# Pairs of tiles in a Strassen feed-forward: their input combinations taken apart into two halves, decode rows first, two products of the second column block ahead of the first block's third

## The chip, the cores and the metric

The kernel runs on one core of a Trainium2 chip. The metric is the device time of one execution in microseconds (us). Five engines work beside each other, each with its own in-order instruction queue: TensorE (PE; PEld is its weight load), VectorE (DVE), ScalarE (ACT), GpSimd (POOL) and SyncE (SP, which here only issues DMAs). The order of each queue is fixed when the program is built, by a planner that works from the order of the program text and from estimated times; an instruction then waits in its queue for the semaphores of what it needs.

## The reference, cut to what matters

Two layers of an encoder work on 1,024 prompt rows and 128 decode rows (8 streams of 16), together 9 tiles of 128 rows by 1,024 columns. A layer is a mixer, an output projection with a norm, and a gated feed-forward with a causal convolution of width 3:

```python
x = layer_norm(ALPHA * x + (mix @ w_out), ln1_g, ln1_b)
hg = x @ w_gate
hu = x @ w_up
ext = jnp.concatenate([conv_prev, hg], axis=1)
conv = conv_b + sum(conv_w[j] * ext[:, j:j + t] for j in range(CONV_W))
x = layer_norm(ALPHA * x + (jax.nn.gelu(conv) * hu) @ w_down, ln2_g, ln2_b)
```

`w_gate` and `w_up` are 1,024 by 2,816. All is float32 and has to stay nearly exact, so each operand is split in a high part (a cast to TensorE's float32r) and a low part (the operand less its high part), and each product is three matmuls (`mm3`, lines 176 to 178): high by high, high by low, low by high.

## The kernel before

**The feed-forward as seven products.** The two weights of a block of 128 columns (`f` = 0 to 21) and the two halves of the rows form a 2 by 2 block product, done in Winograd's form of Strassen with seven products in place of eight: A11 by B11, A12 by B21, S2 by T2, S1 by T1, S4 by B22, S3 by T3, A22 by T4. The A and S are weights and sums of weights, made anew for each block. The B and T are inputs, made once for each layer: B11 and B21 are the two column halves of tiles 0 to 3 and half of the decode tile, B22 is the second column half of tiles 5 to 8 and the other half of the decode tile, and the T combine them. The first row half is in tiles 0 to 3 (group `G1` with the decode tile 4), the second in tiles 5 to 8 (`G2`); tile `j` of the second is paired with tile `j - 5` of the first. Each operand is 128 by 4 by 576, high and low; `product` (line 1379) makes one product in 24 matmuls of 288 columns, each k-step by the three of `mm3`, into one PSUM tile of two banks out of four such tiles (`banks`).

**Before the feed-forward.** The output projection goes over four column slabs; with the last (`s` = 3) each tile of G2 is normalised (`norm_rows`, then `affine_rows`: line 233 multiplies by the gain, line 234 adds the bias, on the two engines that `NORM1` names for the tile) and stored to `x1d`. `VP` means multiply on DVE and add on POOL, `VV` both on DVE. The decode tile and tiles 0 to 3 were turned (transposed by TensorE) and split by `half1` while the projection still ran.

**The pairs.** `pair(j, where)` turns tile `j` (line 1238, eight matmuls, into a PSUM tile named trx, halves va and vb), copies va into a buffer t3 (line 1276), and makes t1 = va - B11 by two POOL subtractions (lines 1261 and 1262; high part, then low part), B22 from vb, t2 = vb - t1 and t3 = vb - va on DVE (lines 1279, 1280), T1 and T2 by splitting t1 and t2 (`put`: line 1228 on ACT makes the high part, line 1229 the low part), t2 = B21 - t2 by two POOL operations (lines 1266, 1267), and T3 and T4 by splitting t3 and t2. The three buffers t1 (in `tail`), t2 and t3 are the same for all four pairs. `pair_dec` does the same for the decode rows on POOL, with the same buffers, after the four pairs. In the text, product A11 of block 0 stands ahead of the pairs, A12 of block 0 between the second and third pair, and everything else after `pair_dec`.

**Weights.** `wnext` makes the next weight operand of a list `wops` in the order of use and splits it (line 1341 on ACT, 1342 on DVE) into one of eight slots of `ring`; the slots are handed round, so one is free when the product that used it is over. The sums S take POOL operations (lines 1335 to 1337 for S2, of which the first writes `tail` and S1 is split from it; line 1339 for S4). Raw weights come by SP in halves of 512 KB (`raw_load`) into two buffers. Eight `wnext` come ahead of the pairs, and each product later calls one more.

**The loop over blocks.** For each `f`: seven products; s1 is copied from the first (line 1502), `gate_in` and `add` take the others out of PSUM on DVE, `conv` and `gated` finish the block, and it is stored to `ad`. The down-projection loads it again from there (`load_a`, two buffers).

Of the kernel before, what the change touches and what calls it, by code (L numbers as in the profile page):

```python
# [10 lines left out]
F32 = mybir.dt.float32  # L11
# [10 lines left out]
P = 128  # L22
# [7 lines left out]
NF = 22  # L30
# [37 lines left out]
def hybrid_encoder(ctx: ExitStack, tc: tile.TileContext, d: dict):  # L68
    nc = tc.nc
# [64 lines left out]
    plan = []  # L134
    MOVER = nc.vector
    PP, VV, VP = (nc.gpsimd, nc.gpsimd), (nc.vector, nc.vector), (nc.vector, nc.gpsimd)
    NORM1 = 5 * [VP] + 4 * [VV]
    NORM2 = [6 * [VP] + 3 * [VV], 8 * [VP] + [VV]]
    for L in range(d["layers"]):
        plan.append((d["w_v"][L], nc.vector if L == 0 else nc.gpsimd))  # L140
# [49 lines left out]
    tail = arp.tile([P, 640], F32, name="tail")  # L190
# [83 lines left out]
    for L in range(d["layers"]):  # L274
# [13 lines left out]
        for q, tl in enumerate(SETS):  # L288
            n = len(tl)
# [542 lines left out]
        for p in range(3):  # L832
# [16 lines left out]
            st = {}  # L849
# [293 lines left out]
        xp1 = pool(f"xp1_{L}", 1, st=fst)  # L1143
        hx = xp1.tile([P, 1170], F32, name="hx")
        ct = [xp1.tile([P, 1152], F32, name="ct0")]
        xg1s = ExitStack()
        xpg = pool(f"xpg_{L}", 1, st=xg1s)
        for j in G1:
# [50 lines left out]
        arb = opr.tile([P, 4608], F32R, name="arb")  # L1199
        xs2 = ExitStack()  # L1200
        xp2 = pool(f"xp2_{L}", 1, st=xs2, right=True)
        temps = [tail[:, 0:512]] + [xp2.tile([P, 512], F32, name=f"temp{n}") for n in range(2)]
        x12d = xp2.tile([P, 4, 2, 32], F32, name="x12d")
        for j in G2:
            x1s[j] = xp2.tile([P, D], F32, name=f"x1_{j}")
            nc.sync.dma_start(x1s[j], x_src[j])
# [3 lines left out]
        def operand(t, n):  # L1210
            return t[:, 4608 * n:4608 * n + 4608].rearrange("p (a k n) -> p a k n", a=2, k=4)

        opx = {"B11": operand(ar, 0), "B21": operand(ar, 1), "T3": operand(ar, 2), "T4": operand(ar, 3),
               "B22": operand(ara, 0), "T1": operand(arb, 0)}
        def temp():
            temps.append(temps.pop(0))
            return temps[-1]

        def cols_of(i):

            if i < 4:
# [4 lines left out]
        def put(at, n, src, eng):  # L1226

            nc.scalar.copy(at(n, 0), src)  # L1228
            eng.tensor_tensor(at(n, 1), src, at(n, 0).bitcast(F32), ALU.subtract)

        def turned_x(src, where):

            out = []
            for c in range(2):
                b = where(c)
                bv = b.rearrange("p (k t) -> p k t", k=4)
                for k in range(4):
                    nc.tensor.transpose(bv[:, k, :], src[:, (4 * c + k) * P:(4 * c + k + 1) * P], ident)
                out.append(bv)
            return out  # L1240
# [18 lines left out]
        def sub2(at, t, n, src, e):  # L1259

            e[0].tensor_tensor(t, src, at(n, 0).bitcast(F32), ALU.subtract)
            e[1].tensor_tensor(t, t, at(n, 1).bitcast(F32), ALU.subtract)

        def rsub2(at, t, n, src, e):

            e[0].tensor_tensor(t, at(n, 0).bitcast(F32), src, ALU.subtract)
            e[1].tensor_tensor(t, t, at(n, 1).bitcast(F32), ALU.add)
# [2 lines left out]

        def pair(j, where):

            va, vb = turned_x(x1s[j], where)
            at = cols_of(j - 5)
            t1, t2, t3 = (temp().rearrange("p (k t) -> p k t", k=4) for _ in range(3))
            nc.scalar.copy(t3, va)
            sub2(at, t1, "B11", t3, (G, G))
            put(at, "B22", vb, V)
            V.tensor_tensor(t2, vb, t1, ALU.subtract)
            V.tensor_tensor(t3, vb, t3, ALU.subtract)  # L1280
            put(at, "T1", t1, V)
            put(at, "T2", t2, V)
            rsub2(at, t2, "B21", t2, (G, G))
            put(at, "T3", t3, V)
            put(at, "T4", t2, V)

        def pair_dec():
            at = cols_of(4)
            t1, t2, t3 = (temp()[:, :256].rearrange("p (k c t) -> p k c t", k=4, c=2) for _ in range(3))
            sub2(at, t1, "B11", x12d, (G, G))  # L1290
            put(at, "T1", t1, G)
            rsub2(at, t2, "B22", t1, (G, G))
            put(at, "T2", t2, G)
            rsub2(at, t3, "B22", x12d, (G, G))
            put(at, "T3", t3, G)
            rsub2(at, t2, "B21", t2, (G, G))
            put(at, "T4", t2, G)

        def norm1(j):
            if j in G2:  # L1300
# [6 lines left out]
        aw = {}  # L1307
        raws = {}
        wops = [(n, f) for f in range(NF) for n in ("A11", "A12", "S2", "S1", "S4", "S3", "A22")]

        def wslot(k):
            return ring[:, 1024 * k:1024 * k + 512], ring[:, 1024 * k + 512:1024 * k + 1024]

        def raw_load(f, a):
            r = rawp.tile([P, 1184], F32, tag="raw", name="raw")
            nc.sync.dma_start(r[:, :1024], d["w_gu"][L, f, :, 1024 * a:1024 * a + 1024])
            raws[f, 2 * a], raws[f, 2 * a + 1] = r[:, 0:512], r[:, 512:1024]

        def wnext():


            i = wnext.i
            if i == len(wops):
                return
            wnext.i += 1
            n, f = wops[i]
            if n == "A11" and f == 0:
                raw_load(0, 0)
                raw_load(0, 1)
            if n == "A12" and f > 0:  # L1330
                raw_load(f, 1)
            a11, a12, a21, a22 = (raws.get((f, c)) for c in range(4))
            src = {"A11": a11, "A12": a12, "S1": tail[:, 0:512], "S2": a11, "S3": a21, "S4": a12, "A22": a22}[n]
            if n == "S2":
                G.tensor_tensor(tail[:, 0:512], a21, a22, ALU.add)
                G.tensor_tensor(a21, a11, a21, ALU.subtract)
                G.tensor_tensor(a11, tail[:, 0:512], a11, ALU.subtract)
            if n == "S4":
                G.tensor_tensor(a12, a12, a11, ALU.subtract)
            h, l = wslot((4 + i) % 8)  # L1340
            nc.scalar.copy(h, src)  # L1341
            V.tensor_tensor(l, src, h.bitcast(F32), ALU.subtract)  # L1342
            aw[n, f] = h.rearrange("p (k n) -> p k n", k=4), l.rearrange("p (k n) -> p k n", k=4)
            if n == "S4" and f < NF - 1:
                raw_load(f + 1, 0)

        wnext.i = wnext.late = 0

# [15 lines left out]
        t2p = pool(f"t2p{L}", 1, st=fst)  # L1364
        art = t2p.tile([P, 4608], F32R, name="art")
        opx["T2"] = operand(art, 0)
        for _ in range(4):
            wnext()
        pst.close()
# [29 lines left out]
        def where():  # L1399
            t = banks("trx")  # L1400
            return lambda c: t[:, c, :]

        first = [product("A11", 0, "B11")]
        pair(5, where())
        pair(6, where())
        first.append(product("A12", 0, "B21"))
        pair(7, where())
        pair(8, where())
        pair_dec()
        turn1.clear()  # L1410
        for _ in range(wnext.late):
            wnext()
# [5 lines left out]
        nc.sync.dma_start(stc, d["st_conv"][L])  # L1418
        tails = fp.tile([P, NF, 16], F32, name="tails")
        tailp = fp.tile([P, NF, 2], F32, name="tailp")  # L1420
        as_ = ExitStack()
        asp = pool(f"as{L}", 2, st=as_, right=True)
        gs_ = ExitStack()
        gsp = pool(f"gs{L}", 1, st=gs_, right=True)
        ct.append(gsp.tile([P, 1152], F32, name="ct1"))
        s1, s2, s3 = (gsp.tile([P, 2, 288], F32, name=n) for n in ("s1", "s2", "s3"))
        nc.gpsimd.memset(hx[:, 0:2], 0.0)

        def halves_of(t, h):
# [35 lines left out]
        def load_a(f):  # L1465
            o = 2304 * ((f + 2) % 8)
            ah, al = ar[:, o:o + 1152], ar[:, o + 1152:o + 2304]
            for c in range(2):
                s_ = slice(576 * c, 576 * c + 576)
                rw = asp.tile([P, 576], F32, tag="araw", name="araw")  # L1470
                nc.sync.dma_start(rw, ad[f][:, s_])
                nc.scalar.copy(ah[:, s_], rw)  # L1472
                V.tensor_tensor(al[:, s_], rw, ah[:, s_].bitcast(F32), ALU.subtract)
            avs[f] = (ah, al)
# [19 lines left out]

        for f in range(NF):
            end = f == NF - 1
            b1, b2 = first if f == 0 else (product("A11", f, "B11"), product("A12", f, "B21"))
            if end:
                load_a(0)
                load_w(0, 0)  # L1500
            G.tensor_copy(dv[:, :, 0:2], stc[:, f, :].rearrange("p (b t) -> p b t", b=8))
            nc.scalar.copy(s1, b1[:, :, :288])
            gate_in(f, 0, s1, b2)
            add(s1, s1, product("S2", f, "T2"))
            if end:
                load_a(1)
                load_w(0, 1)
            add(s2, s1, product("S1", f, "T1"))
            gate_in(f, 1, s2, product("S4", f, "B22"))
            conv(f)  # L1510
            b7 = product("S3", f, "T3")
            add(s2, s2, b7)
            add(s3, s1, b7)
            gated(f, 1, s2)
            add(s3, s3, product("A22", f, "T4"))
            gated(f, 0, s3)
            nc.scalar.dma_start(ad[f], ct[f % 2])


        gs_.close()  # L1520
        as_.close()
        ops_.close()
        pst.close()
        pst = ExitStack()
# [3 lines left out]
        ws_ = ExitStack()  # L1528
        ac1 = pool(f"ac1_{L}", 1, st=ws_, right=True)
        acc = [(ac1 if j in G1 else ac2).tile([P, D], F32, name=f"acc{j}") for j in range(NT)]  # L1530
        asp = pool(f"at{L}", 2, st=ws_, right=True)
        wsp = pool(f"ws{L}", 1, st=ws_, right=True)
        wdv["x"] = wsp.tile([P, 4 * 1024], F32R, name="wdx")
        gt, bt = hx[:, :D], ct[0][:, :D]
# [231 lines left out]
```

## Time and profile before

| | |
|---|---|
| time, median of 3 runs | 2965.39 us (2965.12 to 2967.64) |
| profiled execution, its own time | 2963.75 us |
| its span in the trace | 2961.9 us |
| PE busy | 2791.9 us, 94% of the span |
| PE weight load busy | 2616.6 us, 88% |
| DVE busy | 2072.2 us, 70% |
| ACT busy | 1375.6 us, 46% |
| POOL busy | 937.4 us, 32% |
| mean granted clock of PE | 0.972 of full speed |

The table is to be read as a sum over stages: a share of 94% means that PE stood still for 170 us of the span, and where these lie is not in the table. The page's 40 slices (74 us each) show PE at 9 tenths or more but for a few, among them the one around 700 us and the one around 2170 us, which hold the pairs of the first and of the second layer.

### The profile page before, as it was taken

What the parts mean: (1) busy time and instruction counts of PE and PEld (TensorE: products, weight loads), DVE (VectorE), ACT (ScalarE), POOL (GpSimd) and SP (SyncE); (2) the same over time, 40 slices, a digit from 0 to 9 for tenths busy, and PEclk for the clock granted to TensorE, in tenths of its full rate; (3) what the DMA queues carried; (4) which work ended last, traced back from release to release, by engine and by line L of the source; (5) the groups of instructions that cost most, each with busy time, mean ns of one, the idle gap of its engine ahead of it and who ended that gap; (6) DMA issues with size and microseconds to landing.
All of it is one profiled execution on the core that took longest, in us unless ns stands there. A gap on an engine that the chain in (4) does not pass through costs nothing.

```text
span 2961.9 us, 51451 instructions
## 1 busy us (share of the span) xinstructions
PE 2791.9 (94%) x19412; PEld 2616.6 (88%) x19412; DVE 2072.2 (70%) x4706; ACT 1375.6 (46%) x2881; POOL 937.4 (32%) x927
## 2 busy tenths in 40 slices
PE   9999999994999999999998999989959999999998
PEld 8888898994999999788898988989959999997886
DVE  6899778765666666554678996787656666665646
ACT  6588556543333333411255884666433333334211
POOL 3334443445223222000433455334352322310003
PEclk9999999997999999999999999999979999999999
DMA  4111123131222222533112111131312222234411
GB/s 139 53 60 48 41 65 105 53 132 45 75 78 72 75 75 87 165 129 111 72 51 83 36 53 39 54 112 53 132 45 75 75 75 74 76 104 139 160 64 64
DMA packets 100981, 239.95 MB, mean 81 GB/s; under 512 B 20710, under 2 KB 41086, under 8 KB 100734
## 3 DMA queue, kind: packets, MB, share of 16 engines
q1 hardware_dynamic: 83982, 195.38, 20.4%
q10 hardware_dynamic: 16752, 41.29, 3.6%
q8 instruction: 153, 2.51, 0.3%
q14 instruction: 94, 0.77, 0.1%
HBM read 181.99 MB, written 54.64 MB: 80 GB/s over the span
## 4 chain that ended last, share of the span: by engine, by line
PE 77%; DVE 11%; DMA 3%; issue 3%; POOL 3%; ACT 2%; SPq 0%; ACTq 0%; DVEq 0%; POOLq 0%
PE pg L178 11%; PE pg L176 11%; PE pg L177 11%; PE pdn L176 6%; PE pdn L178 6%; PE pdn L177 6%; PE pwo L176 2%; PE pwo L178 2%; PE pwo L177 2%; PE pvg L176 2%; PE pvg L177 2%; PE pvg L178 2%; PE tp L989 1%; DVE spare L562 1%; DMA raw<-w_d 1%
## 5 line engine op out<-in xcount | busy, mean ns | idle before, releaser
L176 PE MATMUL pg<-ar,ring 128*128 128x288 f32 x1408 | 414.6, 294 | 1.1 <-DVE x L1160 1.1
L178 PE MATMUL pg<-ar,ring 128*128 128x288 f32 x1408 | 415.3, 295 | 0.0
L177 PE MATMUL pg<-ar,ring 128*128 128x288 f32 x1408 | 414.5, 294 | 0.0
L1341 ACT CAST ring<-raw 128x512 fp32r<-128x512 f32 x264 | 163.6, 620 | 454.8 <-PE pg L177 417.9
L128 POOL TENSOR_TENSOR ring<-raw,ring 128x512 fp32r<-128x512 f32 (+1 forms) x140 | 193.7, 1409 | 323.2 <-ACT ring L127 275.6
L1342 DVE TENSOR_TENSOR ring<-raw,ring 128x512 fp32r<-128x512 f32 x264 | 204.5, 775 | 110.5 <-ACT ring L1341 106.9
L568 ACT ACTIVATE spare<-sc,cand 128x384 bf16<-128x384 f32 (+4 forms) x262 | 244.3, 932 | 74.7 <-DVE cand L594 30.4
L176 PEld LDWEIGHTS pg<-ar,ring 128*128 128x128 f32 x1408 | 264.1, 188 | 1.3 <-issue 1.3
L178 PEld LDWEIGHTS pg<-ar,ring 128*128 128x128 f32 x1408 | 264.1, 188 | 0.0
L177 PEld LDWEIGHTS pg<-ar,ring 128*128 128x128 f32 x1408 | 264.1, 188 | 0.0
L1597 DVE TENSOR_TENSOR acc<-acc,pdn 128x512 f32<-128x512 f32 x180 | 122.8, 684 | 179.3 <-PE pdn L178 178.0
L1493 DVE TENSOR_TENSOR s<-s,pg 128x576 f32<-128x576 f32 x220 | 164.2, 748 | 53.6 <-PE pg L178 50.9
L1437 DVE TENSOR_TENSOR hx<-s,pg 128x512 f32<-128x512 f32 x88 | 60.5, 688 | 154.5 <-PE pg L178 153.1
L176 PE MATMUL pwo<-ring,ar 128*128 128x256 f32 x576 | 167.1, 290 | 0.0
L178 PE MATMUL pwo<-ring,ar 128*128 128x256 f32 x576 | 164.0, 285 | 0.0
L177 PE MATMUL pwo<-ring,ar 128*128 128x256 f32 x576 | 164.0, 285 | 0.0
L562 DVE TENSOR_SCALAR_CACHE_REDUCE spare<-sc,cand 128x384 bf16<-128x384 f32 (+3 forms) x208 | 158.2, 761 | 1.4
L176 PE MATMUL pg<-art,ring 128*128 128x288 f32 x352 | 104.5, 297 | 51.1 <-ACT art L1228 51.1
L1472 ACT CAST ar<-araw 128x576 fp32r<-128x576 f32 x88 | 58.9, 675 | 198.7 <-PE pdn L177 107.0
L176 PE MATMUL pdn<-ring,ar 128*128 128x512 f32 x360 | 140.9, 391 | 2.9 <-DVE s L1493 2.9
L178 PE MATMUL pdn<-ring,ar 128*128 128x512 f32 x360 | 140.8, 391 | 0.0
L177 PE MATMUL pdn<-ring,ar 128*128 128x512 f32 x360 | 140.7, 391 | 0.0
(403 smaller groups left out, 9533.5 us busy)
## 6 DMA issues: line engine op xcount, KB each, us to landing
raw<-w_gu SPq DMA_DIRECT2D x88, 512.0 KB, 3.7
ad<-ct ACTq DMA_DIRECT2D x44, 576.0 KB, 2.8
araw<-ad SPq DMA_DIRECT2D x88, 288.0 KB, 3.6
raw<-w_d SPq DMA_DIRECT2D x44, 512.0 KB, 4.4
raw<-w_s SPq DMA_DIRECT2D x40, 512.0 KB, 3.9
raw<-w_o SPq DMA_DIRECT2D x32, 512.0 KB, 4.1
x1d<-x ACTq DMA_DIRECT2D x18, 512.0 KB, 2.7
ml<-mixd SPq DMA_DIRECT2D x18, 320.0 KB, 3.2
```

The lines of the kernel that those rows point to most:

```text
L128: eng.tensor_tensor(l[:, t], raw[:, r], h[:, t].bitcast(F32), ALU.subtract)
L176: nc.tensor.matmul(out, lh, rh, start=first, stop=False)
L177: nc.tensor.matmul(out, lh, rl, start=False, stop=False)
L178: nc.tensor.matmul(out, ll, rh, start=False, stop=last)
L562: nc.vector.tensor_scalar(junkv[:, :w], sc[i], cand[q][:, c:c + 1].bitcast(F32), float(kof(i) - w), op0=ALU.is_lt, op1=ALU.add, accum_out= ...
L568: nc.scalar.activation(junka[:, :w], sc[i], AF.Sign, bias=cand[q][:, c:c + 1].bitcast(F32), scale=-1.0, accum_out=dst)
L1341: nc.scalar.copy(h, src)
L1342: V.tensor_tensor(l, src, h.bitcast(F32), ALU.subtract)
L1437: V.tensor_tensor(hp.rearrange("p (c n) -> p c n", c=2), prompt(sv), prompt(b), ALU.add)
L1472: nc.scalar.copy(ah[:, s_], rw)
L1493: V.tensor_tensor(out, a, b[:, :, :288], ALU.add)
L1597: V.tensor_tensor(acc[j][:, cs], acc[j][:, cs], po, ALU.add)
```

## The change

It takes the pairs' work apart and moves it. `pair` now ends after T2 and T1 and returns a function `rest` (B21 - t2, and T3 and T4), which is called after all four pairs. t1 stays in `tail`; t2 and t3 of the first pair are two new buffers, those of each later pair are the two halves of the tile of the pair before. For the last pair (`j` = 8) the two subtractions for t1 are on DVE. `pair_dec` moves ahead of the pairs, into the end of the output projection, with a buffer of its own (x4d); its T3 and T4 splits follow the pairs. Products A11 and A12 of block 1 are made between the pairs, and `wops` has their weights third and fourth; the raw weights come in another order, and the half that holds A11 and A12 of block 1 is read twice. s1 is copied right after the first product and has a place of its own. The bias adds of tiles 5, 6 and 7 go from DVE to POOL. In the down-projection one of `load_a`'s two buffers is s1.

```diff
-    NORM1 = 5 * [VP] + 4 * [VV]
+    NORM1 = 8 * [VP] + [VV]
...
+        s1 = xp1.tile([P, 2, 288], F32, name="s1")
...
-            t1, t2, t3 = (temp().rearrange("p (k t) -> p k t", k=4) for _ in range(3))
+            t1, t2, t3 = (t.rearrange("p (k t) -> p k t", k=4) for t in (tail[:, 0:512], *temps))
+            temps[:] = x1s[j][:, 0:512], x1s[j][:, 512:1024]
+            e = V if j == 8 else G
             nc.scalar.copy(t3, va)
-            sub2(at, t1, "B11", t3, (G, G))
+            sub2(at, t1, "B11", t3, (e, e))
             put(at, "B22", vb, V)
             V.tensor_tensor(t2, vb, t1, ALU.subtract)
             V.tensor_tensor(t3, vb, t3, ALU.subtract)
+            put(at, "T2", t2, V)
             put(at, "T1", t1, V)
-            put(at, "T2", t2, V)
-            rsub2(at, t2, "B21", t2, (G, G))
-            put(at, "T3", t3, V)
-            put(at, "T4", t2, V)
+
+            def rest():
+                rsub2(at, t2, "B21", t2, (G, G))
+                put(at, "T3", t3, V)
+                put(at, "T4", t2, V)
+
+            return rest
 
         def pair_dec():
             at = cols_of(4)
-            t1, t2, t3 = (temp()[:, :256].rearrange("p (k c t) -> p k c t", k=4, c=2) for _ in range(3))
+            t1 = tail[:, :256].rearrange("p (k c t) -> p k c t", k=4, c=2)
             sub2(at, t1, "B11", x12d, (G, G))
             put(at, "T1", t1, G)
-            rsub2(at, t2, "B22", t1, (G, G))
-            put(at, "T2", t2, G)
-            rsub2(at, t3, "B22", x12d, (G, G))
-            put(at, "T3", t3, G)
-            rsub2(at, t2, "B21", t2, (G, G))
-            put(at, "T4", t2, G)
+            rsub2(at, x4d, "B22", t1, (G, G))
+            put(at, "T2", x4d, G)
+            rsub2(at, x12d, "B22", x12d, (G, G))
+            rsub2(at, x4d, "B21", x4d, (G, G))
+
+        def rest_dec():
+            at = cols_of(4)
+            put(at, "T3", x12d, G)
+            put(at, "T4", x4d, G)
...
+        wops[2:9] = wops[7:9] + wops[2:7]
...
-            if n == "A11" and f == 0:
+            if i == 0:
+                raw_load(1, 0)
                 raw_load(0, 0)
-                raw_load(0, 1)
-            if n == "A12" and f > 0:
-                raw_load(f, 1)
...
+            if i == 3:
+                raw_load(0, 1)
             if n == "S4" and f < NF - 1:
                 raw_load(f + 1, 0)
+            if n == "A22" and f < NF - 1:
+                raw_load(f + 1, 1)
...
+        pair_dec()
         for _ in range(4):
             wnext()
...
-        first = [product("A11", 0, "B11")]
-        pair(5, where())
-        pair(6, where())
-        first.append(product("A12", 0, "B21"))
-        pair(7, where())
-        pair(8, where())
-        pair_dec()
+        first = {f: [] for f in range(2)}
+        rests = []
+
+        def early(f, n, x):
+            first[f].append(product(n, f, x))
+
+        early(0, "A11", "B11")
+        nc.scalar.copy(s1, first[0][0][:, :, :288])
+        rests.append(pair(5, where()))
+        early(0, "A12", "B21")
+        rests.append(pair(6, where()))
+        early(1, "A11", "B11")
+        rests.append(pair(7, where()))
+        early(1, "A12", "B21")
+        rests.append(pair(8, where()))
+        rest_dec()
+        for r in rests:
+            r()
...
-                rw = asp.tile([P, 576], F32, tag="araw", name="araw")
+                rw = s1.rearrange("p c n -> p (c n)") if f > 1 and c else asp.tile([P, 576], F32, tag="araw", name="araw")
```

## Rows read from the trace of the kernel before

**Rows 1.** Waits of PE, 655 to 725 us: total us, times, longest.

```profile
PE pg L176 <- ACT art L1228: 25.6, 1, 25.6
PE trx L1238 <- ACT art L1228: 12.5, 2, 7.7
```

**Rows 2.** Stretches: length, busy (count) of PE, PEld, DVE, ACT, POOL; clock, DMA, GB/s.

```profile
680.00:700.00 20.00, 1.94 (x8) 1.56 (x8) 12.57 (x20) 8.46 (x15) 11.40 (x9) 0.50 0.00 0
700.00:720.00 20.00, 10.85 (x64) 10.86 (x65) 6.51 (x8) 5.69 (x11) 16.34 (x19) 0.64 0.01 2
720.00:740.00 20.00, 20.00 (x152) 20.00 (x152) 15.23 (x24) 9.01 (x13) 7.14 (x7) 1.00 0.32 111
```

**Rows 3.** Timeline of PE: start, us, instruction, [idle before].

```profile
662.11 1.95 PE L1238 MATMUL trx<-identr,x 128*128 128x128 f32 x16
...
671.97 1.94 PE L1238 MATMUL trx<-identr,x 128*128 128x128 f32 x8 [4.74 <-ACT art L1228]
...
709.15 0.61 PE L176 MATMUL pg<-art,ring 128*128 128x288 f32 x1 [25.57 <-ACT art L1228]
...
733.87 0.29 PE L176 MATMUL pg<-art,ring 128*128 128x288 f32 x1
...
2183.38 0.61 PE L176 MATMUL pg<-art,ring 128*128 128x288 f32 x1 [25.56 <-ACT art L1228]
...
2208.25 0.29 PE L176 MATMUL pg<-art,ring 128*128 128x288 f32 x1
```

**Rows 4.** Timeline of ACT in the same stage.

```profile
645.45 0.62 ACT L1341 CAST ring<-tail 128x512 fp32r<-128x512 f32 x1 [0.71 <-PE pwo L177]
...
674.85 0.59 ACT L1276 COPY temp<-trx 128x512 f32<-128x512 f32 x1 [2.37 <-DVE ar L1229]
...
683.38 0.59 ACT L1276 COPY temp<-trx 128x512 f32<-128x512 f32 x1 [1.23 <-DVE ar L1229]
...
708.69 0.41 ACT L1228 CAST art<-temp 128x256 fp32r<-128x256 f32 x1 [2.31 <-POOL temp L1267]
```

**Rows 5.** Timeline of DVE.

```profile
672.35 1.21 DVE L234 TENSOR_TENSOR x<-x,ct 128x1024 f32<-128x1024 f32 x1
...
675.96 0.69 DVE L1229 TENSOR_TENSOR ara<-trx,ara 128x512 fp32r<-128x512 f32 x1 [1.20 <-ACT ara L1228]
679.01 1.09 DVE L1229 TENSOR_TENSOR ar<-temp,ar 128x512 fp32r<-128x512 f32 x1 [2.36 <-ACT ar L1228]
680.20 0.69 DVE L1279 TENSOR_TENSOR temp<-trx,tail 128x512 f32<-128x512 f32 x1
680.81 0.68 DVE L1280 TENSOR_TENSOR temp<-trx,temp 128x512 f32<-128x512 f32 x1
...
699.06 0.69 DVE L1229 TENSOR_TENSOR art<-temp,art 128x512 fp32r<-128x512 f32 x1
```

**Rows 6.** Timeline of POOL.

```profile
613.84 2.40 POOL L234 TENSOR_TENSOR x<-x,ct 128x1024 f32<-128x1024 f32 x1 [4.24 <-DVE x L233]
...
640.33 1.29 POOL L1335 TENSOR_TENSOR tail<-raw 128x512 f32<-128x512 f32 x1 [17.87 <-DMA raw<-w_gu]
...
650.77 0.55 POOL L212 TENSOR_TENSOR bnsc<-bnsc,mhalf 128x1 f32<-128x1 f32 x1 [0.45 <-DVE bnsc L211]
...
665.32 1.34 POOL L1261 TENSOR_TENSOR tail<-temp,ar 128x512 f32<-128x512 f32 x1 [1.66 <-ACT temp L1276]
...
675.85 1.26 POOL L1261 TENSOR_TENSOR tail<-temp,ar 128x512 f32<-128x512 f32 x1
677.07 1.25 POOL L1267 TENSOR_TENSOR temp<-temp,ar 128x512 f32<-128x512 f32 x1
678.29 1.26 POOL L1262 TENSOR_TENSOR tail<-tail,ar 128x512 f32<-128x512 f32 x1
...
701.96 0.72 POOL L1262 TENSOR_TENSOR tail<-tail,ar 128x256 f32<-128x256 f32 x1
```

**Rows 7.** DMA issues, 600 to 760 us: KB each, median us to landing.

```profile
raw<-w_gu SPq DMA_DIRECT2D x8, 512.0 KB, 3.8
```

More of the change, by code (lines that the diff above doesn't have):

```diff
@@ L1201, in hybrid_encoder @@
         xp2 = pool(f"xp2_{L}", 1, st=xs2, right=True)
-        temps = [tail[:, 0:512]] + [xp2.tile([P, 512], F32, name=f"temp{n}") for n in range(2)]
-        x12d = xp2.tile([P, 4, 2, 32], F32, name="x12d")
+        x12d, x4d = (xp2.tile([P, 4, 2, 32], F32, name=n) for n in ("x12d", "x4d"))
         for j in G2:
@@ L1214, in hybrid_encoder @@
                "B22": operand(ara, 0), "T1": operand(arb, 0)}
-        def temp():
-            temps.append(temps.pop(0))
-            return temps[-1]
         def cols_of(i):
@@ L1366, in hybrid_encoder @@
         opx["T2"] = operand(art, 0)
+        xpt = pool(f"xpt_{L}", 1, st=xs2, right=True)
+        temps = [xpt.tile([P, 512], F32, name=f"temp{n}") for n in range(2)]
+        pair_dec()
         for _ in range(4):
@@ L1420, in hybrid_encoder @@
         tailp = fp.tile([P, NF, 2], F32, name="tailp")
-        as_ = ExitStack()
-        asp = pool(f"as{L}", 2, st=as_, right=True)
         gs_ = ExitStack()
@@ L1425, in hybrid_encoder @@
         ct.append(gsp.tile([P, 1152], F32, name="ct1"))
-        s1, s2, s3 = (gsp.tile([P, 2, 288], F32, name=n) for n in ("s1", "s2", "s3"))
+        s3, s2 = (gsp.tile([P, 2, 288], F32, name=n) for n in ("s3", "s2"))
+        as_ = ExitStack()
+        asp = pool(f"as{L}", 2, st=as_, right=True)
         nc.gpsimd.memset(hx[:, 0:2], 0.0)
@@ L1496, in hybrid_encoder @@
             end = f == NF - 1
-            b1, b2 = first if f == 0 else (product("A11", f, "B11"), product("A12", f, "B21"))
+            b1, b2 = first[f] if f < 2 else (product("A11", f, "B11"), product("A12", f, "B21"))
             if end:
@@ L1501, in hybrid_encoder @@
             G.tensor_copy(dv[:, :, 0:2], stc[:, f, :].rearrange("p (b t) -> p b t", b=8))
-            nc.scalar.copy(s1, b1[:, :, :288])
+            if f:
+                nc.scalar.copy(s1, b1[:, :, :288])
             gate_in(f, 0, s1, b2)
@@ L1517, in hybrid_encoder @@
             nc.scalar.dma_start(ad[f], ct[f % 2])
+        as_.close()
         gs_.close()
-        as_.close()
         ops_.close()
@@ L1530, in hybrid_encoder @@
         acc = [(ac1 if j in G1 else ac2).tile([P, D], F32, name=f"acc{j}") for j in range(NT)]
-        asp = pool(f"at{L}", 2, st=ws_, right=True)
+        asp = pool(f"at{L}", 1, st=ws_, right=True)
         wsp = pool(f"ws{L}", 1, st=ws_, right=True)
```

## The prediction

> **What bounds the kernel now.** I read the page first. PE is busy 94% of the span, so what can be won lies where it stands still, and two of the 40 slices hold most of that, one in each layer. Then the waits of PE in the first of these stretches: two entries make 38.1 us, both put down to ACT's split of the second block's inputs, 12.5 us ahead of turns (the transposes of a pair) and 25.6 us ahead of the first product of T2 [rows 1]. Then the stretches: between 680 and 700 us PE works 1.94 of 20 us, at half its clock; at 720 us it is full again and stays so [rows 2]. Last the timelines. The reader should see in PE's that the last turn stands 25.57 us ahead of the product S2 by T2 at 709.15, that S2 of the next block starts at 733.87, and that the second layer does the same 1474.2 us later (2183.38, 2208.25) [rows 3]. So this is one stage that occurs twice, and I cost it once and double it.
>
> What sets its length is a serial chain. A pair's copy of va waits for the split of the pair before, as its buffer is the same: 674.85, then 683.38, 8.53 us for each pair [rows 4]. The last T2 split of pair 8 starts at 699.06 [rows 5]; after it come the decode rows, whose T2 has its high part at 708.69 [rows 4], and S2 by T2 follows at once.
>
> **A second limit, behind the chain.** POOL's operations on 512 columns are 1.25 us long and start 1.22 apart, those on 256 take 0.72, the bias add on 1,024 takes 2.40 [rows 6]. On DVE a split takes 0.69, and successive starts are 0.6 apart [rows 5]. But look at DVE's split at 679.01: 1.09 us, and it ends at 680.10, 0.55 after POOL's operation that began at 678.29 is over. Its inputs are both in SBUF. The one at 675.96 reads PSUM and SBUF and takes its 0.69 though POOL works all that time [rows 5, 6]. I read this as: a DVE operation with two SBUF inputs and a POOL operation don't run at once. The Trainium skill ("SBUF — State Buffer", Who interferes with whom) says so outright: a DVE instruction with two SBUF inputs and a GpSimd instruction that reads SBUF exclude each other for the whole instruction. It speaks against a change that runs the two engines beside each other; this trace agrees with it at 679.01 (1.09 against 0.69). Read as a rule it makes the later S2 by T2 of the two that are worked out below (693 against 684).
>
> **The change, part by part** (layer 1's times stand for both).
>
> *Decode rows first.* Ten POOL operations of 0.72 and their casts go from behind the pairs to about 640 us, where POOL has been idle for 17.87 us [rows 6]. That cover gone, they would cost 7.2 us. From the end of the chain they take the stretch from the end of T2 of pair 8 (699.75) to 709.15, 9.4 us.
>
> *Sums S of block 0 later.* The raw half with A21 and A22 is now read after A12 of block 1 is split, in the last of the four slots to come free, at 645.45 [rows 4]. With 0.6 for ACT, 0.6 to 2 for DVE and 3.8 to land [rows 7] POOL starts on them at about 652, not 640. Nothing waits for them before S2 by T2.
>
> *What must be done before S2 by T2.* From 652 on, in the shared reading, POOL and DVE's two-SBUF operations are one queue, with the durations of [rows 5, 6]. Up to pair 7's t1 it holds: four sums S at 1.25, 5.0; three reciprocal roots of norms at 0.55, 1.6; bias adds of tiles 5 to 7, three at 2.40, 7.2; t1 of pairs 5 to 7, six at 1.25, 7.5; on DVE four gain multiplies and one bias add at 1.2, 6.0; five weight splits at 0.6, 3.0; T1 and T2 low parts of pairs 5 and 6, 2.4. That is 32.7 us, to 684.7. PSUM has four tiles; while A12 of block 0 and A11 and A12 of block 1 are held there is one left, so the turns of pair 8 wait for pair 7's t2 and t3. From there the chain is t2 and t3 (0.6 + 0.7), turns (1.0 at full clock, half of the 1.95 for sixteen; 1.94 at half clock [rows 3]), copy 0.6, t1 on DVE 1.3, t2 0.7, T2's high part 0.6 and low part 0.7: 6.2 to 7.1, with handovers 6.5, to 691.2. I add 2 us for gaps and for parts of the rests that are put in between: S2 by T2 at 693. Bounds: 684 if nothing excludes anything, 703 if the pairs keep their period (both worked out under the rivals).
>
> *Bias adds to POOL.* They free DVE of 3.6 us, and take 3 times 2.40 on POOL [rows 5, 6]; in the shared reading that is 3.6 us lost, else up to 3.6 won. I take the loss; it is in the sum.
>
> *Two products moved.* A11 and A12 of block 1 go into PE's idle time; a product is 24 matmuls, 3.16 us at 152 in 20 us [rows 2]. Before, from 709.15 to 733.87 there are 24.7 us for seven products, 22.1 of them at full clock, so 2.6 went to the half clock after the idle stretch. PE idles again ahead of S2 by T2 (8 to 10 us after A12 of block 1), so I take the same 2.6: five products in 18.4 us, and S2 of block 1 at 711.4.
>
> *The rests.* Four rests at 2.5 on POOL and 1.2 on DVE, 14.8, and 1.4 for the decode rows. Some 6 us of that fit into the chain's gaps between 684 and 693. The other 10 are done at about 704; T4 is needed by A22 at 693 + 15.2 = 708. Then the sums for S2 of block 1 (3.75, and 1.25 for S4): 709, split by 710.5. No stall, but no room either; without the 6 us in the gaps S2 of block 1 would be 5 us later.
>
> *Held PSUM.* A11 and A12 of block 1 stay in two of the four tiles during block 0, and its five products share the others; a `conv` ahead of an `add` in DVE's queue can hold one. I take 1.5 us: S2 of block 1 at 713. Bounds 0 and what the rival below gives.
>
> *At nothing.* The early copy of s1 is moved, on an ACT that is busy 8.46 of 20 us [rows 2]. The half that is read twice is 512 KB in 3.8 us [rows 7] on a DMA share of 0.00 [rows 2]; if it were late, S2 of block 1 would be up to 3.8 later. The raw halves of later blocks wait for the same buffers as before. `load_a` still alternates between two buffers. Order of pools: addresses only.
>
> *Sum.* S2 of block 1 goes from 733.87 to 713, 21 us a layer; from there on both kernels do the same work. Two layers: 42 us. 2963.75 - 42 = 2922 for an execution like the profiled one; the median of the runs is 1.6 us above that one, so 2923.
>
> **Rivals.**
>
> *Free overlap.* The two engines disturb each other little, and the pairs run at the pace of `tail`: from 665.32 [rows 6], t1 2.5, t2 and t3 1.3, T1's split 0.9, so 4.7 a pair; pair 7's t1 is there at 677.2, and with 6.5 S2 by T2 starts at 684, S2 of block 1 at 702.4. 31.5 us a layer, 2902; with no half clock behind it 2897. For it: the splits and rests are short, and the planner may order them well. Against it: the 1.09.
>
> *The period stays.* One buffer `tail`, PSUM and interleaved POOL operations (1261, 1267, 1262 in turn at 675.85 to 678.29 [rows 6]) leave each pair at 8.53, and the POOL adds put the norms 3.6 later. T2 of pair 8 then ends at 703.4 instead of 699.75; plus 18.4 and 1.5, 723. 11 us a layer, 2943. For it: rests fill POOL between the two subtractions of t1. Against it: they stand behind in the text.
>
> *PSUM starves the products* (slower). The five products of block 0 wait in turn for one of two tiles, whose readers on DVE stand behind splits and `conv`. It eats the gain of 21 us when each of the five waits 4.2 us, more than the 3.16 that a product takes; at 6 us each it is 30 lost, 9 us a layer slower, 2983. Against it: DVE takes a product out in one 0.7 us operation.
>
> **How the numbers follow.** The forecast, bounded by the shared path of POOL and DVE and with 15 to 28 us a layer (2909 to 2935), gets 0.58. Free overlap 0.20. The period stays 0.14, of which a fifth ends within 0.2% (6 us, about what this kernel's measurement can tell from no change). PSUM starves 0.05, and 0.03 for a planner's order that gains nothing. Faster: 0.58 + 0.20 + 0.11 + a small part of the rest, 0.90. Same 0.05. Slower 0.05. The range takes in most of both neighbours: 2897 to 2945.
>
> **What would show it.** Right: decode T2 split before 660; the pairs' t1 less than 7 us apart; a second pair of products of block 1 before 690; S2 by T2 near 693 after less than 12 us of idle PE; DVE splits of more than 1 us beside POOL's; next S2 near 713. Free overlap shows splits at 0.69 throughout and S2 by T2 before 687. If the period stays, t1 starts are 8 us apart. PSUM as the cause shows waits of PE for DVE `add` or `gate_in` between the five products. The prediction falls if S2 by T2 is not ahead of 705, or if S2 of block 1 starts more than 24 us after it.

## The result, and the profile after

The kernel after takes 2921.2 us (median of four, 2919.34 to 2925.24); beside it on the same chip the kernel before took 2966.29. The ratio is 0.985, with a 95% interval of 0.9833 to 0.9867: 45 us faster, and 2 us from the 2923 that was forecast. Its profiled execution took 2922.04 us, span 2920.2.

The total came out, but it is not made of the parts that the forecast added up. The stretches of the stage come first (length; busy and count of PE, PEld, DVE, ACT, POOL; clock, DMA share, GB/s), to be laid beside [rows 2]:

```profile
660.00:680.00 20.00, 13.97 (x88) 13.76 (x88) 18.18 (x23) 7.47 (x11) 14.80 (x11) 0.83 0.37 132
680.00:700.00 20.00, 8.76 (x52) 7.82 (x52) 17.05 (x22) 9.29 (x17) 15.35 (x11) 0.73 0.12 38
700.00:720.00 20.00, 17.08 (x113) 16.88 (x114) 18.73 (x25) 8.84 (x15) 11.86 (x9) 0.85 0.17 53
```

PE works 8.76 us from 680 to 700 instead of 1.94, at a granted clock of 0.73 instead of 0.50. The column that matters for the rest of this text is the third: DVE was busy 12.57 and 6.51 us in the second and third stretch; now it is busy 17 to 19 of every 20. Busy counts an instruction from its start to its end, what it waits for the other engine in between included. The waits of PE from 655 to 725 us (total us, times, longest) show six entries, 20.8 us together, in the place of the two of [rows 1] with 38.1:

```profile
PE pg L176 <- ACT art L1224: 5.9, 1, 5.9
PE pg L176 <- DVE x L1279: 3.9, 1, 3.9
PE pg L176 <- DVE x L1161: 3.9, 1, 3.9
PE trx L1234 <- ACT art L1224: 3.2, 1, 3.2
PE trx L1234 <- DVE hx L1462: 3.1, 1, 3.1
PE pg L176 <- DVE s L1516: 0.8, 1, 0.8
```

Four of the six are ended by DVE, where ACT's split ended nearly all before. PE's timeline, to be laid beside [rows 3]:

```profile
659.01 0.28 PE L178 MATMUL pwo<-ring,ar 128*128 128x256 f32 x1
...
663.14 0.58 PE L176 MATMUL pg<-ar,ring 128*128 128x288 f32 x1 [3.85 <-DVE x L1161]
...
695.00 0.58 PE L176 MATMUL pg<-art,ring 128*128 128x288 f32 x1 [5.93 <-ACT art L1224]
...
702.08 0.58 PE L176 MATMUL pg<-arb,ring 128*128 128x288 f32 x1 [3.86 <-DVE x L1279]
...
705.34 0.44 PE L176 MATMUL pg<-art,ring 128*128 128x288 f32 x1
...
707.29 0.29 PE L177 MATMUL pg<-art,ring 128*128 128x288 f32 x1
...
719.42 0.29 PE L176 MATMUL pg<-art,ring 128*128 128x288 f32 x1
...
2170.20 0.29 PE L176 MATMUL pg<-art,ring 128*128 128x288 f32 x1
```

The product S2 by T2 starts twice. Its first twelve matmuls, one half of the columns (tiles 5 and 6 and half of the decode rows), run from 695.00 although pair 8 is not done; the other half begins with one matmul at 705.34 and runs on from 707.29. S2 of block 1 starts at 719.42, in the second layer at 2170.20.

I measure the stage from the end of the last `pwo` matmul ahead of it (659.29 here, 657.71 before) to S2 of block 1: 60.1 us, against 76.2. In the second layer it is 60.3 against 76.5. So the stage gives 16.1 us a layer in the mean, not 21. The rest came from a place that the forecast had put down at nothing. In the first rows here, of the kernel before, the down-projection starts and comes to the weights kept in `art`; the next two are the same matmuls after:

```profile
1196.97 0.47 PE L176 MATMUL pdn<-ring,ar 128*128 128x512 f32 x1 [0.85 <-DVE s L1493]
...
1228.03 0.79 PE L176 MATMUL pdn<-art,ar 128*128 128x512 f32 x1 [4.09 <-ACT acc L1595]
```

```profile
1181.52 0.39 PE L176 MATMUL pdn<-ring,ar 128*128 128x512 f32 x1
...
1206.97 0.51 PE L176 MATMUL pdn<-art,ar 128*128 128x512 f32 x1 [0.34 <-ACT acc L1619]
```

31.06 us became 25.45; a wait of 4.09 for ACT's copy out of PSUM is down to 0.34. In the second layer 29.51 became 26.89, and from S2 of block 1 to the first of these matmuls 463.1 and 464.3 became 462.1 and 462.1. Down-projection and its lead-in: 5.6 + 2.6 + 1.0 + 2.2 = 11.4 us. With the stage's 32.3 that is 43.7; the spans differ by 41.7, and 2 us went the other way elsewhere (1.6 of them ahead of the stage).

### The profile page after: what moved, and what is told of

Its sections match the earlier page's. It is cut to its first block, busy times and chain, and to the rows that moved or that the text cites. A ratio compares the mean times of both kernels' runs of the same rounds, so it can differ in the third digit from the quotient of the medians.

```text
span 2920.2 us, 51433 instructions
## 1 busy us (share of the span) xinstructions
PE 2795.3 (96%) x19412; PEld 2619.0 (90%) x19412; DVE 2089.0 (72%) x4704; ACT 1373.5 (47%) x2881; POOL 958.9 (33%) x929
## 3 DMA queue, kind: packets, MB, share of 16 engines
q1 hardware_dynamic: 84270, 196.43, 20.8%
## 4 chain that ended last, share of the span: by engine, by line
PE 75%; DVE 14%; issue 4%; DMA 3%; ACT 2%; POOL 2%; SPq 0%; ACTq 0%; DVEq 0%; POOLq 0%
PE pg L176 11%; PE pg L178 11%; PE pg L177 11%; PE pdn L178 5%; PE pdn L176 5%; PE pdn L177 5%; PE pwo L176 2%; PE pwo L177 2%; PE pwo L178 2%; PE pvg L176 2%; PE pvg L177 2%; PE pvg L178 2%; DVE spare L562 1%; PE tp L989 1%; DMA raw<-w_d 1%
## 5 line engine op out<-in xcount | busy, mean ns | idle before, releaser
L1465 ACT ACTIVATE ct<-hx,cwt 128x512 f32<-128x512 f32 x88 | 71.9, 816 | 131.6 <-DVE hx L1460 126.9
L1474 POOL COPY tailp<-hx 128x2 f32<-128x2 f32 x44 | 30.3, 689 | 313.2 <-DVE hx L1460 313.2
```

The lines of the kernel that those rows point to most:

```text
L1465: nc.scalar.activation(cf[:, 512 * h:512 * h + 512], hp, AF.Identity, **kw)
```

## Experiments

All are compared with the kernel before on the same chip, whose median was between 2962.6 and 2967.6 in the three groups of runs. "The stage" is always from the end of `pwo` to S2 of block 1, layer 0 first; it was 60.1 and 60.3 after, 76.2 and 76.5 before.

**E2 and E2c: the down-projection by itself.** Both start from the kernel before. E2 takes over the three edits behind the stage: s1 out of the pool of the loop's buffers and one of the two load buffers, the other order of two pools, and one buffer fewer in the down-projection:

```
-        as_ = ExitStack()
-        asp = pool(f"as{L}", 2, st=as_, right=True)
+        s1 = fp.tile([P, 2, 288], F32, name="s1")
         gs_ = ExitStack()
...
+        as_ = ExitStack()
+        asp = pool(f"as{L}", 2, st=as_, right=True)
...
-                rw = asp.tile([P, 576], F32, tag="araw", name="araw")
+                rw = s1.rearrange("p c n -> p (c n)") if f > 1 and c else asp.tile([P, 576], F32, tag="araw", name="araw")
...
+        as_.close()
         gs_.close()
-        as_.close()
...
-        asp = pool(f"at{L}", 2, st=ws_, right=True)
+        asp = pool(f"at{L}", 1, st=ws_, right=True)
```

> The kernel before with only the second part of the edit that touches the down-projection: s1 outside the pool of the loop's buffers, the two pools in the other order, one of the two load buffers being s1. If the 5.6 us that the changed kernel gains at the start of the down-projection in each layer come from this part, 2954 to 2960 us, and the first product of the second group of blocks stands some 25.5 us behind the first one of the first group instead of 31.1. If they come from what the feed-forward left behind (queues that the pairs' change had emptied earlier), 2965 to 2968 us.

Measured: 2955.02 us, ratio 0.9958 (0.9941 to 0.9974), 12.5 us faster, with the stage at 76.3 and 76.2. At the start of the down-projection and its lead-in it gains 11.4 us in the two layers, as the kernel after does. E2c keeps only the exchanged order of the two pools; within one of them s1, s2 and s3 lie the other way round.

> The kernel before with nothing but the order of the two pools behind the pairs exchanged (E2 without the staging of the gate weights in s1 and the smaller pool at the down-projection). Theory, addresses: the weights of the down-projection land where something earlier is free, and all of E2's gain is there: 2954 to 2960. Rival, the transfers of the gate weights through s1 are what starts them earlier: within 3 us of before.

Measured: 2954.3 us, ratio 0.9956 (0.9942 to 0.9971), 11.7 us faster; the stage is at 75.8 and 76.4. By the medians the order of the pools alone gives as much as all three edits. Place by place it is less: the start of the down-projection and its lead-in give 7.6 of the 12.8 us by which the span of E2c's profiled execution is shorter. The wait for the copy is short here too:

```profile
1195.17 0.47 PE L176 MATMUL pdn<-ring,ar 128*128 128x512 f32 x1
...
1222.78 0.49 PE L176 MATMUL pdn<-art,ar 128*128 128x512 f32 x1 [0.71 <-ACT acc L1595]
```

In the kernel before, ACT's timeline shows what was late:

```profile
1226.08 0.62 ACT L1488 CAST ring<-raw 128x512 fp32r<-128x512 f32 x1 [2.48 <-DMA raw<-w_d]
1226.82 0.67 ACT L1472 CAST ar<-araw 128x576 fp32r<-128x576 f32 x1
1227.39 0.58 ACT L1595 COPY acc<-pdn 128x512 f32<-128x512 f32 x1
```

A weight cast waits 2.48 us for its transfer, and the copy that PE needs at 1228.03 stands behind it on the same engine. In E2c its counterpart waits 0.70, and only behind the matmul at 1222.78. The larger difference is in ACT's casts of the activations that are loaded again. Their waits, of the kernel before from 1197 to 1232 us and of E2c from 1195 to 1230:

```profile
ACT ar L1472 <- DMA araw<-ad: 7.7, 5, 3.6
```

```profile
ACT ar L1472 <- DMA araw<-ad: 0.8, 2, 0.4
```

In E2c these casts hardly stand in ACT's queue waiting for data, ahead of the copies out of PSUM. That other addresses let the transfers be issued in another rhythm is what the edit leaves as the cause; which buffer's release does it is not shown.

**E5: decode rows last.** `pair_dec()` goes back behind the pairs.

```
-        pair_dec()          # ahead of the first four weight slots
...
         rests.append(pair(8, where()))
+        pair_dec()
         rest_dec()
```

> The changed kernel with the decode rows' combination behind the four pairs again. If its ten POOL operations and their casts stand in idle time at 640 us now and on the path behind the pairs before, it costs the 9.4 us a layer that the prediction gave it, less what other waits hide: 2930 to 2940 us. If the planner lifts it to the front by itself, as all it needs is ready at 640, within 3 us of 2921.

Measured: 2947.32 us, ratio 0.9945 (0.9924 to 0.9967); stage 73.0 and 73.7. It takes back 26.1 us, 13 a layer: more than the expectation (2930 to 2940) and the forecast (9.4 a layer) gave it.

```profile
707.68 0.61 PE L176 MATMUL pg<-art,ring 128*128 128x288 f32 x1 [21.68 <-ACT art L1224]
```

PE stands still 21.68 us in one piece. Each half of the columns holds decode rows, so with them last no half of S2 by T2 can start early; with them first twelve matmuls of it and thirteen of the next product run in what was one wait. The 9.4 did not count that.

**E3, E9a and E9: early products, the early copy, a second buffer for t1.** E3 is the kernel after with only block 0's two products ahead, and the old order of weights and of their loads. E9a is E3 with s1 copied where it was before; E9 is E9a with two buffers for t1 in turn.

```
-        first = {f: [] for f in range(2)}
+        first = {f: [] for f in range(1)}
...
-        early(1, "A11", "B11")
...
-        early(1, "A12", "B21")
```

```
-            t1, t2, t3 = (t.rearrange("p (k t) -> p k t", k=4) for t in (tail[:, 0:512], *temps))
+            t1, t2, t3 = (t.rearrange("p (k t) -> p k t", k=4) for t in (t1s[j % 2], *temps))
...
+        t1s = [tail[:, 0:512], xpt.tile([P, 512], F32, name="tone")]
```

> The changed kernel without the two early products of block 1 and with the weights in the old order. If they fill time in which TensorE stands still anyway, they are worth their 6.3 us a layer less what the PSUM tiles that they hold cost (the 3.86 us wait for the last reader of pair 8's turns goes): 2926 to 2934 us. The rival, that the pairs' own rate sets the start of the next block and the products are hidden either way: within 3 us of 2921.

> Control for the next one: without the early products of block 1 and without the early copy of s1, whose 2.3 KB a partition make room for another buffer. The first product then stays in PSUM, as before the change. If nothing in it waits for a PSUM tile, within 3 us of 2923; if the held tile delays pair 7's turns, up to 2932.

> The control with two buffers for t1, used in turn. In the changed kernel t1 of pair 6 starts 0.08 us after the split that frees the buffer, and so does that of pair 7. If this buffer sets the pace of the pairs, t1 of pair 6 now starts within 4 us of pair 5's, the first product of T2 is 3 to 6 us earlier, and the time 6 to 12 us under the control's. If POOL and DVE's turn-taking sets it, within 3 us of the control.

Measured: E3 2922.78 us (0.9851, 0.9836 to 0.9866), E9a 2924.1 (0.9864, 0.9847 to 0.9882), E9 2922.78 (0.9865, 0.9845 to 0.9886). All three are within 3 us of the kernel after, and no two can be told apart. The stage is 62.0 in E3 and 60.9 in E9 (layer 0). The two products of the second column block are worth 1.6 us by the medians, 1.9 and 1.6 in the two layers by the stage. In E9 `tail` is no longer handed on, but t1 of pair 6 starts 7.30 us after that of pair 5, where the expectation asked for 4 at most and the kernel after has 7.66. PE's waits from 655 to 725 us have moved:

```profile
PE trx L1233 <- ACT art L1223: 10.8, 2, 9.1
PE pg L176 <- ACT art L1223: 8.2, 1, 8.2
```

**E4: t1 on DVE for every pair.**

```
-            e = V if j == 8 else G
+            e = V
```

> The changed kernel with t1 of all four pairs on DVE (0.6 us for each subtraction instead of 1.25 on POOL). If the two engines take turns, six operations save 0.6 us each, about 3.9 us a layer, and t1 starts of successive pairs come closer than the 6.6 to 8.0 us of now: 2911 to 2917 us. If DVE as the full engine sets the rate, it gets 3.6 us a layer more to do: 2924 to 2930 us.

Measured: 2924.89 us, ratio 0.9863 (0.9846 to 0.9879); stage 63.6 and 63.9. Taking six instructions off POOL gained nothing; the time is in the range of the rival, that DVE is the full engine.

**E6 and E10: the rests, and the sets of buffers.** E6 calls each rest right behind its pair; E10 does so too and lets all pairs share one t2 and t3.

```
-        rests.append(pair(5, where()))
+        pair(5, where())()
...
-            temps[:] = x1s[j][:, 0:512], x1s[j][:, 512:1024]     # E10 alone
```

> The changed kernel with each pair's rest called right behind the pair. If the order of the text decides, each rest (two POOL operations and two splits) stands ahead of the next pair's t1, and the pair period goes from 6.6 to 8.0 back towards 8.5: 2928 to 2945 us. If the rests fill gaps whatever their place, as POOL has them one by one between other pairs' operations already: within 4 us of 2921.

> The kernel after with the rests written right behind each pair, and one set of t2 and t3 for all pairs, as before the change. Theory: a pair's copy of va waits again for the last split of the pair before, the period goes from 7.4 back to 8.5 us or more, and the rest of a pair stands in the chain of the next: 3 to 6 us a layer, 2928 to 2934. Rival: sharing between POOL and DVE sets the period anyway, as a second buffer for t1 and the place of the rests in the text changed nothing: within 4 us of 2921.

Measured: E6 2921.0 us (0.9858, 0.984 to 0.9875): where the text puts the rests doesn't matter. E10 2932.6 (0.9884, 0.9868 to 0.9901), stage 66.0 and 69.3: the second set of buffers is worth 11.4 us, 5.7 a layer (by the stage 5.9 and 9.1), as the theory had it. Its pairs run at the old pace on POOL, 684.10, 692.65: 8.55 apart, the 8.53 of [rows 4]:

```profile
684.10 1.27 POOL L1257 TENSOR_TENSOR tail<-temp,ar 128x512 f32<-128x512 f32 x1
...
692.65 1.27 POOL L1257 TENSOR_TENSOR tail<-temp,ar 128x512 f32<-128x512 f32 x1
```

**E14: eight POOL instructions fewer.** The kernel leaves out the subtractions that make T4; T4 is then the split of T2.

```
             def rest():
-                rsub2(at, t2, "B21", t2, (G, G))
```

> The kernel after without the two POOL subtractions of the four rests (T4 of tiles 5 to 8 is then the split of T2 and not of T2's difference): 8 instructions, 10 us of POOL alone and some 13 us as they run beside DVE, less in each layer. Theory, the stage is as long as what POOL and DVE share: the stage of 60 us gets 5 to 9 us shorter in each layer, 2903 to 2911. Rival, the chain of turns, t1 and splits sets it and the rests lie beside it: within 4 us of 2921.

Measured: 2919.16 us, ratio 0.9834 (0.9819 to 0.985); stage 58.3 and 58.3. Eight POOL instructions, of 1.26 to 1.72 us in the kernel after, 12.5 us a layer, were gone, and the stage was 2 us shorter. The theory, that it is as long as the work that POOL and DVE share, fell, and the time is in the range of its rival, that the chain of turns, t1 and splits sets the stage. That chain runs through DVE's queue. In the stretches of E14 and then of E9 DVE (the third column) has no gap:

```profile
680.00:700.00 20.00, 10.48 (x53) 9.58 (x54) 19.97 (x28) 11.33 (x21) 7.15 (x5) 0.75 0.11 38
```

```profile
680.00:700.00 20.00, 7.22 (x30) 6.51 (x31) 20.00 (x25) 10.66 (x19) 14.39 (x9) 0.50 0.11 36
```

With POOL relieved (E14) or `tail` doubled (E9) DVE is busy 19.97 and 20.00 of 20 us, and the stage is within 2 us of 60. E4's DVE stands at 19.90 in that stretch. In E10, whose chain of buffers is the limit, it is at 12.63. But busy is not work. Some of it is still waiting for POOL, in E14 too:

```profile
683.73 1.77 DVE L1225 TENSOR_TENSOR ar<-temp,ar 128x512 fp32r<-128x512 f32 x1
...
689.51 3.42 DVE L1225 TENSOR_TENSOR ar<-x,ar 128x512 fp32r<-128x512 f32 x2
```

These three splits and one of 1.16 (686.02) take 3.6 us more than four of 0.68. So DVE's own work fills about 16 of E14's 20 us, and turn-taking is a part of what is left.

**E1 and E16: bias adds back on DVE.** E1 puts the adds of tiles 5 to 7 back; E16 is E1 with pair 8's rest on DVE.

```
-    NORM1 = 8 * [VP] + [VV]
+    NORM1 = 5 * [VP] + 4 * [VV]
...
-                rsub2(at, t2, "B21", t2, (G, G))     # E16 alone
+                rsub2(at, t2, "B21", t2, (e, e))
```

> The changed kernel with the bias adds of tiles 5 to 7 on DVE again (1.2 us each instead of 2.4 on POOL). If POOL and DVE's operations with two SBUF inputs take turns, the adds on POOL cost 1.2 us each and hold DVE's queue, so that the first product waits 3.85 us for the last row of the output projection: without them that wait falls under 1.5 us, pair 5's t1 starts at least 3 us earlier than 674.3, and the time is 2912 to 2919 us. The rival, that DVE is simply the full engine here and gains by what POOL takes over: 2924 to 2930 us, t1 of pair 5 later.

> E1's kernel (bias adds of tiles 5 to 7 on DVE, 2939.65 us) with the two subtractions of pair 8's rest on DVE instead of POOL. Theory, head of the line: E1 lost its time because DVE's fixed order put the T4 split of pair 8, which waits 3.05 us for POOL's subtraction, and two weight splits behind it ahead of the add that frees the PSUM tile. With the subtractions on DVE nothing there waits for POOL: 4 to 7 us less in each layer, 2926 to 2932. Rival, DVE has too much to do: E1's 3.6 us of bias adds are what it lost, and 1.4 us more on DVE makes it worse: 2938 to 2946.

Measured: E1 2939.65 us, ratio 0.9906 (0.9891 to 0.992); stage 69.7 and 67.3. Both expectations missed: three bias adds on DVE instead of POOL cost 18.4 us, 9.2 a layer (by the stage 9.5 and 7.1). Much of it is one place. DVE's timeline of E1:

```profile
713.16 1.09 DVE L1225 TENSOR_TENSOR ar<-x,ar 128x512 fp32r<-128x512 f32 x1 [3.05 <-ACT ar L1224]
714.17 2.35 DVE L1347 TENSOR_TENSOR ring<-raw,ring 128x512 fp32r<-128x512 f32 x2
716.45 0.74 DVE L1516 TENSOR_TENSOR s<-s,pg 128x576 f32<-128x576 f32 x1
```

The add at 716.45 empties a PSUM tile for which PE waits 5.64 us. It stands behind pair 8's T4 split, which waits for POOL's subtraction by way of ACT, and behind two weight splits. In the kernel after, the same add comes at 708.95, ahead of that T4 split (710.62): the order in DVE's queue is another. From the end of `pwo` the add comes 54.9 us in, against 49.7. E16 was to cure this, and measured 2936.79 us, ratio 0.9896 (0.9879 to 0.9912), which can't be told from E1. POOL no longer held DVE, but the T4 cast on ACT waited 5.60 us for DVE's own subtraction, with the weight casts queued behind it:

```profile
713.72 0.62 ACT L1224 CAST ar<-x 128x512 fp32r<-128x512 f32 x1 [5.60 <-DVE x L1263]
714.25 2.17 ACT L1346 CAST ring<-raw 128x512 fp32r<-128x512 f32 x4
```

and the add came at 716.79. So the place of E1's loss is shown. That it is the order and not the 3.6 us more for DVE is argued, not shown; E16 hit neither price.

## Why the prediction was right, and where its parts were not

**What held.** Decode rows first: their T2 was split at 647.06 on POOL, ahead of 660. The second product of block 1 was done at 684.85, ahead of 690. The wait ahead of S2 by T2 fell from 25.57 to 5.93. The turn-taking of POOL and DVE, on which the forecast was put between 684 and 703, is plain in the trace: on DVE a split with both inputs in SBUF takes 1.75 beside POOL, while one that reads PSUM keeps its 0.68 though POOL works from 691.82 to 693.53:

```profile
688.99 1.75 DVE L1225 TENSOR_TENSOR ar<-temp,ar 128x512 fp32r<-128x512 f32 x1
...
691.82 1.71 POOL L1258 TENSOR_TENSOR tail<-tail,ar 128x512 f32<-128x512 f32 x1
692.33 0.68 DVE L1225 TENSOR_TENSOR ara<-trx,ara 128x512 fp32r<-128x512 f32 x1
```

POOL's t1 of pairs 5, 6 and 7 are 1.29, 1.67 and 1.64 long:

```profile
674.31 1.29 POOL L1257 TENSOR_TENSOR tail<-temp,ar 128x512 f32<-128x512 f32 x1
...
681.97 1.67 POOL L1257 TENSOR_TENSOR tail<-x,ar 128x512 f32<-128x512 f32 x1 [3.69 <-DVE arb L1225]
...
688.54 1.64 POOL L1257 TENSOR_TENSOR tail<-x,ar 128x512 f32<-128x512 f32 x1 [0.77 <-DVE arb L1225]
```

The rule that the prediction cited from the Trainium skill ("SBUF — State Buffer", Who interferes with whom) agrees with this trace. Free overlap, which needed splits of 0.69 throughout, is out.

**The step that failed: what must be done before S2 by T2.** The sum said that pair 7's t1 is ready at 684.7, 27.0 us after the end of `pwo`; it was ready at 693.53 (the end of POOL's operation at 691.82 above), 34.2 after. The four t1 start 7.66, 6.57 and 8.04 apart, not under 7 as forecast: between the forecast and the old 8.53. The sum took POOL and the two-input work of DVE as the one queue that limits, gave DVE 11.4 us in it, and put the rests behind it. Two things were missing.

The smaller one is the rests. Three of their operations, 4.7 us, run on POOL before pair 7's t1 is ready (683.60, 686.51 and 690.15). In E14, which leaves them out, it is ready 32.0 us after the end of `pwo`, so they are worth about 2.3 of the 7.2 us:

```profile
690.79 1.59 POOL L1258 TENSOR_TENSOR tail<-tail,ar 128x512 f32<-128x512 f32 x1
```

The larger one is DVE's other work. DVE's groups from 653 to 694 in the kernel after show what the sum left out (busy us, mean ns, idle before):

```profile
L228 DVE SCALAR_TENSOR_TENSOR bnsc<-bnmv,bnsc 128x1 f32<-128x1 f32 x4 | 3.8, 944 | 1.6 <-POOL bnsc L212 1.6
...
L220 DVE BATCH_NORM_STATS2 bnst<-x 128x6 f32<-128x512 f32 x4 | 2.7, 686 | 0.1
L1225 DVE TENSOR_TENSOR ara<-trx,ara 128x512 fp32r<-128x512 f32 x4 | 2.7, 682 | 0.0
```

Statistics of the norms, splits of turned halves, t2 and t3, and the residual adds are some 11 us in all. They keep their length beside POOL, but they stand in DVE's one queue with its two-input work. The scales of the norms (L228) have two SBUF inputs and belong in the shared queue: one took 0.10, at 665.72 with POOL idle, another stood 1.74 beside POOL's bias add of 671.88 to 674.35:

```profile
672.62 1.74 DVE L228 SCALAR_TENSOR_TENSOR bnsc<-bnmv,bnsc 128x1 f32<-128x1 f32 x1
```

The forecast asked which instructions exclude each other and not what else stands in the queue of the engine that has most of them. E4, E9 and E14, which relieve POOL or `tail` and leave DVE at 19.9 to 20.0 of 20 us, agree with that; E1, which loads DVE, goes the same way. No run took work off DVE alone, and its busy time holds waits for POOL, so "DVE limits the stage" is what these runs point to and not more; how much of the missing 5 us is DVE's own work and how much turn-taking stays open.

**Two errors that partly cancelled in the stage.** Pair 8's T2 was complete at 704.82, 45.5 us after `pwo`, where 35.3 was forecast: 10.2 late.

```profile
703.05 1.77 DVE L1225 TENSOR_TENSOR art<-x,art 128x512 fp32r<-128x512 f32 x1
```

Of this 7.2 were lost before pair 7's t1 and 3.0 in the chain behind it, which took 11.3 us instead of 8.3: between the two halves of pair 8's t1 (696.58 and 699.93) DVE has a split of a rest, 1.75 long. From the end of that T2 to S2 of block 1 it took 14.6 us and not 20, because half of the first two products had already run at 695.00 and 702.08. The forecast had S2 by T2 wait for the whole of T2. Together they make 60.1 instead of 55.3. By its own terms the stated bound was crossed: S2 of block 1 starts 24.4 us after the first S2 by T2, over 24, since that product starts early and in halves. The waits for PSUM between the products were 3.9 and 0.8, 4.7 together, where 1.5 was forecast.

**Single terms.** Decode rows: 9.4 forecast, 13 measured (E5). Bias adds to POOL: a loss of 3.6 forecast, a gain of 9.2 a layer measured (E1): the sign was wrong. Whether DVE's load or the order of its queue makes it, E16 did not settle. Two products: 1.9 a layer at most (E3), though 6.3 us were moved; the stage's end hardly hangs on them. The rests: no stall behind the pairs, as forecast, and their place in the text is worth nothing (E6), but ahead of S2 by T2 they cost about 2 us a layer (E14). The second set of t2 and t3: 5.7 a layer (E10); the prediction didn't price it by itself, and "the period stays" is what happens without it.

**The pools, costed at nothing.** "Order of pools: addresses only" was the second wrong step. The order gave 11.7 us by itself (E2c), and the edits behind the stage 12.5 together (E2). The forecast's 42 was 10 too much for the stage, and this made it up: 32.3 + 11.4. The number was right by a wrong sum; that the two errors are of one size is luck.

## What to carry to other kernels

Before a shared resource is made the bound, add up everything on each engine that takes part, the work that reads PSUM too: an engine at 17 to 19 of 20 us is the first suspect, and here relieving its neighbours gave 2 us a layer or nothing (E4, E9, E14), while putting 3.6 us of work back on it cost 9.2 a layer, in part by the order of its queue (E1). Then take the waits out of its busy time: a split of 1.75 us that is 0.68 long by itself is mostly waiting. A product that reads its input in column halves starts when its half is there, so what belongs to both halves should be done first (E5: 13 us a layer for 9.4 us of chain). An exchange of two pools is not "addresses only" where buffers are filled by transfers; by itself it is worth 11.7 us (E2c), beside the 45 of the whole change.

## What was not expected of the hardware

POOL and DVE slow each other in both directions: POOL's operations on 512 columns went from 1.29 to 1.64 and 1.67, DVE's from 0.68 to 1.75, so each side pays for the other, and the profile shows the waiting as busy time on both. A gain multiply on 1,024 columns, two SBUF inputs on DVE, took 1896 ns in the mean of four in this stage, the longest 3.43 us, against 1214 in the kernel before.
